# Conditioning vectors of a two-block kernel: second shift and scale as row dot products on VectorE, first gate on TensorE, x loaded feature-major, silu of the conditioning by exp

## The chip, the cores and the metric

One Trainium2 chip; the kernel runs on 1 of its 8 cores. The metric is the device time of one execution in microseconds. The median of three runs of the kernel before is 1270.04 us (1266.39 to 1270.33). The profile is one further execution; its time from the first to the last instruction is called the span.

## The reference

x is 256 tokens by 1024 features, in float32. Only the first block matters here:

```python
cond = silu(c)                                   # c is [1, 1024]
mod = cond @ ada_w + ada_b                       # [1, 6 * 1024]
sh1, sc1, g1, sh2, sc2, g2 = split(mod, 6)
h = rms_norm(x, norm_g[0]) * (1 + sc1) + sh1
x = x + g1 * sb_mixer(h)                         # 16 heads, stick-breaking attention
h = rms_norm(x, norm_g[1]) * (1 + sc2) + sh2
x = x + g2 * hier_moe(h)                         # 32 experts, two for each token
```

The six vectors of the conditioning are products of one row of 1024 with a matrix of 1024 by 6144, 24 MB in all. A second block follows (feed-forward, mixer, feed-forward, last normalization).

## The kernel before

**Tiling.** Activations lie feature-major, as eight tiles of 128 features by 256 tokens. Products that must be exact to float32 are split: a weight w is loaded, ScalarE writes its rounded part wr, VectorE the rest wl = w - wr (split_w), and three matmuls make up for one. Weights come as loads of 1 MB (128 x 2048) into a ring of 15 tiles; the loads are issued by SP's queue in one fixed order, and a load waits until its ring tile is free, with all later loads behind it.

**The first block, in the order of the program.** x is loaded token-major, transposed on TensorE and copied out (L209 to L213); the squares are summed on ScalarE (sq), and the token scales rb spread by two matmuls. cond is a Silu on ScalarE. For each quarter of the features, mod1 forms the first shift and scale (mod_cols: eight matmuls on TensorE with the conditioning as weights, a copy, four transposes, a sum) and then h1; values_quarter makes the values v. Then eight pairs of heads follow, p = 0 to 7: each loads wqk, splits its two halves, makes queries and keys with 48 matmuls (qk), and calls attend for the pair before. attend makes logits z, then takes five passes over 768 columns that alternate: Abs, Exp, Ln on ScalarE, sp on VectorE (L358), the rounded part spr on ScalarE and the rest spl on VectorE (L360), with matmuls of both into z, an Exp, and the product with v; oTr and oTl leave PSUM.

**Conditioning beside the attention.** After the pairs p = 2 to 5, mod_feat(1, p - 2) makes the second shift and scale, and after p = 6 and 7 mod_gate makes the first gate g1, each by mod_cols_ahead: the unit's two loads ada are multiplied by cond, the first on VectorE (four moda passes, L259), the second on GpSimd (L263 to L266: 2048, 1024, 512 and 512 columns), and eight small matmuls add up the partitions.

**After it.** The output product y takes 192 matmuls over the split wo, then come the first residual, the logits of the routing (lt), the routing, and the experts, in eight groups of four. Each group reads 16 loads gu and 8 loads d of 1 MB. The first group's weights are loaded ahead, as far as ring and other tiles have room. The rest of the kernel reads on from the experts' end.

**Order.** Tile's scheduler orders each engine's instructions by its own model of time; engines run their queues in that order and wait for each other by semaphores.

Of the kernel before, what the change touches and what calls it, by code (L numbers as in the profile page):

```python
# [41 lines left out]
def tile_model(ctx: ExitStack, tc: tile.TileContext, a, out, dbg=None):  # L42
# [36 lines left out]
    def hold(name, shape, dt=F32):  # L79
        """A ring tile that takes its place now and not only when its data come."""  # L80
# [33 lines left out]
    zeros = cp.tile([P, 1], F32, name="zeros")  # L114
    V.memset(zeros, 0.0)
# [7 lines left out]
    def rsqrt(v, n, name):  # L123
        """1/sqrt(v) for positive v [128, n]."""
# [63 lines left out]
    def mm_feat(o, wr, wl, hr, hl):  # L188
        """o [128 features, 256] = W^T h, W split [128, 8, 128]."""
# [6 lines left out]
    def mm_tok(o, xr, xl, wr, wl, start, stop):  # L196
        """o [128 tokens, n] += x^T w for one contraction block."""
# [3 lines left out]

    # ---- first normalization
    xT = hold("xT", (P, KT, T))
    for k2 in range(4):
        t = gt(f"xT{k2}", (P, 2, T))
        for tb in range(2):
            for kk in range(2):
# [1094 lines left out]
```

## Time and profile before

| what | value |
|---|---|
| median of three runs | 1270.04 us |
| span of the profiled execution | 1264.9 us |
| PE busy | 1094.0 us (86%) |
| DVE busy | 620.1 us (49%) |
| ACT busy | 450.1 us (36%) |
| POOL busy | 101.4 us (8%) |
| mean granted TensorE clock | 0.938 of full speed |
| HBM traffic | 354.57 MB read |

The page gives no device time of the profiled execution other than its span; the median of the runs is 5.1 us above it. PE is TensorE's matmuls, DVE VectorE, ACT ScalarE, POOL GpSimd, SP the queue that issues the loads. The kernel passes through stretches with different limits: the start and the values to about 51 us, the attention to about 149 us, the output product to about 178 us, routing, the experts from about 191 to 640 us, the second block to the end. Shares of the whole span mix these.

### The profile page before, as it was taken

How to read it: one execution, taken by the hardware profiler on the slowest of the kernel's cores; microseconds unless marked ns; L12 is line 12 of the kernel's file. 1: busy time of each engine (PE TensorE's matmuls, PEld its weight loads, DVE VectorE, ACT ScalarE, POOL GpSimd, SP SyncE). 2: the span in 40 equal slices, each digit the busy share in tenths (PEclk: the TensorE clock that was granted, in tenths of full speed). 3: DMA queues.
4: the chain of work that ended last, by engine and by line, in shares of the span. 5: the costliest groups of instructions: out<-in, count | busy, mean ns of one | idle time of the engine just before them, and what ended most of it. 6: DMA issues, size and time to landing. Idle time of an engine off the chain costs nothing.

```text
span 1264.9 us, 18050 instructions
## 1 busy us (share of the span) xinstructions
PE 1094.0 (86%) x7429; PEld 817.6 (65%) x7429; DVE 620.1 (49%) x1001; ACT 450.1 (36%) x663; POOL 101.4 (8%) x77
## 2 busy tenths in 40 slices
PE   6988988975756776667789999999999999999996
PEld 3787883321312221212179999988988889999995
DVE  4799751210101010101177555577779666755555
ACT  4454641010100000000154444457654555544443
POOL 0277300000000000000020000020000002000001
PEclk9988988989797888978799999999999999999998
DMA  9975688999999999999999440444437656555000
GB/s 382 419 298 219 266 332 357 420 420 420 421 421 418 420 421 421 421 421 422 420 420 370 171 164 1 150 175 159 176 145 296 219 199 250 181 220 182 32 1 34
DMA packets 51354, 356.88 MB, mean 282 GB/s; under 512 B 5824, under 2 KB 6080, under 8 KB 9408
## 3 DMA queue, kind: packets, MB, share of 16 engines
q1 hardware_dynamic: 50400, 353.02, 70.1%
q0 software_dynamic: 576, 2.10, 0.5%
q8 instruction: 61, 1.00, 0.3%
q10 hardware_dynamic: 288, 0.52, 0.1%
q14 instruction: 29, 0.24, 0.1%
HBM read 354.57 MB, written 1.05 MB: 281 GB/s over the span
## 4 chain that ended last, share of the span: by engine, by line
PE 56%; DMA 32%; DVE 7%; issue 2%; ACT 2%; POOL 0%; SPq 0%; ACTq 0%; DVEq 0%
DMA gu<-moe_gu 20%; DMA d<-moe_d 11%; PE fbgu L92 10%; PE fagu L92 9%; PE faacc L92 5%; PE fbacc L92 4%; PE mqk L92 4%; PE mo L92 3%; PE y L92 2%; PE mv L92 2%; PE mz L92 2%; PE mu L92 2%; PE ms L92 2%; PE mg L92 2%; PE gu L92 1%
## 5 line engine op out<-in xcount | busy, mean ns | idle before, releaser
L92 PE MATMUL gu<-gu,xg 128*32 128x512 f32 x1024 | 146.5, 666 | 67.2 <-DMA gu<-moe_gu 67.0
L92 PEld LDWEIGHTS gu<-gu,xg 128*32 128x32 f32 x1024 | 24.8, 113 | 141.0 <-DMA gu<-moe_gu 79.3
L92 PE MATMUL Y<-d,HT 128*32 128x512 f32 (+1 forms) x544 | 83.2, 720 | 26.1 <-DMA d<-moe_d 20.2
L591 DVE TENSOR_SCALAR xg<-xgp,A,mod 128x128 f32<-128x128 f32 x32 | 13.1, 410 | 174.8 <-PE xgp L92 174.8
L656 DVE SCALAR_TENSOR_TENSOR xT<-cmb,g,xT 128x256 f32<-128x256 f32 x60 | 27.8, 484 | 126.4 <-PE cmb L92 126.3
L589 ACT ACTIVATE xg<-xgp,mod,A 128x128 f32<-128x128 f32 x32 | 14.7, 458 | 172.7 <-PE xgp L92 172.7
L92 PEld LDWEIGHTS xgp<-eq,xn 128*128 128x128 f32 x256 | 39.6, 222 | 52.5 <-issue 50.6
L92 PEld LDWEIGHTS Y<-d,HT 128*32 128x32 f32 x544 | 15.5, 126 | 78.7 <-DMA d<-moe_d 50.4
L92 PE MATMUL xgp<-eq,xn 128*128 128x128 f32 x256 | 49.3, 329 | 8.0 <-DVE eq L579 7.1
L650 ACT ACTIVATE Ys<-Y 128x512 f32<-128x512 f32 x15 | 9.0, 597 | 120.0 <-PE Y L92 120.0
L92 PE MATMUL cmb<-CT,Ys 128*128 128x256 f32 x128 | 41.1, 452 | 11.3 <-ACT Ys L650 10.3
L92 PEld LDWEIGHTS cmb<-CT,Ys 128*128 128x128 f32 x128 | 24.9, 217 | 36.7 <-ACT Ys L650 25.3
L849 POOL TENSOR_TENSOR faq<-faq,faq 128x256 f32<-128x256 f32 x10 | 9.3, 951 | 460.6 <-ACT faq L845 460.4
L612 DVE TENSOR_TENSOR H<-H,gu 128x512 f32<-128x512 f32 x8 | 5.5, 688 | 66.7 <-ACT H L611 66.7
L263 POOL TENSOR_TENSOR ada<-ada,cond 128x2048 f32<-128x2048 f32 x6 | 24.5, 4079 | 33.9 <-DMA ada<-ada 33.9
L611 ACT ACTIVATE H<-gu 128x512 f32<-128x512 f32 x8 | 4.8, 597 | 60.2 <-PE gu L92 60.2
L970 DVE SCALAR_TENSOR_TENSOR cv<-cs,pk,cv 128x255 f32<-128x255 f32 (+2 forms) x48 | 22.3, 477 | 0.4
L615 PEld LDWEIGHTS HTp<-kc,H 128*128 128x128 f32 x32 | 4.8, 188 | 25.3 <-DVE H L612 25.3
L782 DVE TENSOR_TENSOR fbsc<-fbgu,rb 128x512 f32<-128x512 f32 x22 | 15.0, 691 | 10.9 <-PE fbgu L92 10.8
L782 DVE TENSOR_TENSOR fasc<-fagu,rb 128x512 f32<-128x512 f32 x22 | 15.0, 690 | 10.5 <-PE fagu L92 10.5
L1204 POOL TENSOR_TENSOR fin<-x,final_norm_g 128x512 f32<-128x512 f32 x4 | 5.1, 1281 | 180.2 <-issue 177.2
L264 POOL TENSOR_TENSOR ada<-ada 128x1024 f32<-128x1024 f32 x6 | 19.1, 3184 | 0.2
(2266 smaller groups left out, 3608.2 us busy)
## 6 DMA issues: line engine op xcount, KB each, us to landing
gu<-moe_gu SPq DMA_DIRECT2D x127, 1024.0 KB, 19.8
d<-moe_d SPq DMA_DIRECT2D x60, 1024.0 KB, 19.8
ada<-ada SPq DMA_DIRECT2D x24, 1024.0 KB, 10.6
fawi<-f1i SPq DMA_DIRECT2D x21, 1024.0 KB, 17.4
fbwi<-f2i SPq DMA_DIRECT2D x21, 1024.0 KB, 4.8
fawo<-f1o SPq DMA_DIRECT2D x11, 1024.0 KB, 14.2
fbwo<-f2o SPq DMA_DIRECT2D x11, 1024.0 KB, 4.8
wqk<-sbqk SPq DMA_DIRECT2D x8, 1024.0 KB, 16.4
```

The source lines that it names most:

```text
L92: return PE.matmul(o, l, r, start=start, stop=stop, **kw)
L263: G.tensor_tensor(w4, w4, cond[:, 4:8, None].to_broadcast([P, 4, 512]), ALU.mult)
L264: G.tensor_tensor(w[:, 0:1024], w[:, 0:1024], w[:, 1024:2048], ALU.add)
L589: S.activation(xg[:, k, :], t, AF.Identity, scale=A2[:, k:k + 1], bias=sh2[:, k:k + 1])
L591: V.tensor_scalar(xg[:, k, :], t, A2[:, k:k + 1], sh2[:, k:k + 1], ALU.mult, ALU.add)
L612: V.tensor_tensor(H, H, gu[:, 1, :], ALU.mult)
L650: S.activation(Ys, Y, AF.Copy)
L656: V.scalar_tensor_tensor(xT[:, kt, :], c[:, kk, :], g2[:, kt:kt + 1], xT[:, kt, :], ALU.mult, ALU.add)
L782: V.tensor_tensor(gu, ps, rb[:, None, :].to_broadcast([P, 2, T]), ALU.mult)
L849: (V if i and kt > 3 else G).tensor_tensor(sums[i], sums[i], s_, ALU.add)
L970: V.scalar_tensor_tensor(cv[:, d:T], ts[:, 0:T - d], pk[:, cw + 3 - d:cw + 4 - d], cv[:, d:T], ALU.mult, ALU.add)
L1204: G.tensor_tensor(z[:, half(hf)], xs, fn[:, half(hf)], ALU.mult)
```

## The change

Five edits, all ahead of the experts.

1. **Second shift and scale.** The matrix is loaded transposed (adar, eight loads of 1 MB, one for each 128 output features, with the 1024 inputs along the columns). A new tile crow holds c, broadcast to all 128 partitions by one DMA of 512 KB, and its silu. Each of the sixteen outputs of 128 features is one VectorE pass over 1024 columns that multiplies and sums (mod_row, accum_out). One adar load and two such passes follow each pair of heads p = 0 to 7. mod_rows_end adds the bias and forms A2 for all features at once.
2. **First gate.** mod_gate(0, h) goes through mod_cols on TensorE, after p = 3 and p = 5. mod_cols_ahead is gone, and with it all its work on GpSimd and VectorE.
3. **x** is loaded feature-major straight into xT; the transposes are gone. The sums of squares come from two ScalarE passes over 1024 columns, one VectorE sum and four matmuls with ones, and lie on all partitions at once, so that rsqrt runs on 128 x 256 in place of 128 x 2.
4. **silu** is c / (1 + exp(-c)), for cond (128 x 8) and crow (128 x 1024): an Exp on ScalarE, an addition, a reciprocal and a product on VectorE. The table for Exp and Ln is loaded first; the Silu table and the second load of it at the start are gone.
5. The first loads are pk, xT, kc in place of kc, x, pk.

```diff
+    set_exp = S.preload_act_table_set("natural_log_exp_and_others")
+    def silu_of(dst, src, e):
+        with tc.issue_after(set_exp.ins):
+            S.activation(e, src, AF.Exp, scale=-1.0)
+        V.tensor_scalar(e, e, 1.0, None, ALU.add)
+        V.reciprocal(e, e)
+        V.tensor_tensor(dst, src, e, ALU.mult)
...
-    def mod_cols_ahead(u, name):
-        acc = acp.tile([P, 512], F32, tag="acc", name=f"moda{name}")
-        ws = [load(a["ada"][u, r], f"ada{u}{r}") for r in range(2)]
-        for j in range(4):
-            V.scalar_tensor_tensor(acc, ws[0][:, 512 * j:512 * j + 512], cond[:, j:j + 1],
-                                   acc if j else zeros.to_broadcast([P, 512]), ALU.mult, ALU.add)
-        w = ws[1]
-        w4 = w.rearrange("p (j n) -> p j n", j=4)
-        G.tensor_tensor(w4, w4, cond[:, 4:8, None].to_broadcast([P, 4, 512]), ALU.mult)
-        G.tensor_tensor(w[:, 0:1024], w[:, 0:1024], w[:, 1024:2048], ALU.add)
-        G.tensor_tensor(w[:, 0:512], w[:, 0:512], w[:, 512:1024], ALU.add)
-        G.tensor_tensor(acc, acc, w[:, 0:512], ALU.add)
...
+    def mod_row(kt):
+        if not crow:
+            c = w8("crow", (P, 2, D))
+            nc.sync.dma_start(c[:, 0], bass.AP(tensor=a["c"].tensor, offset=a["c"].offset, ap=[[0, P], [1, D]]))
+            silu_of(c[:, 0], c[:, 0], c[:, 1])
+            crow.append(c)
+        c = crow[0]
+        w = load(a["adar"][kt], f"adar{kt}")
+        for j in range(2):
+            V.scalar_tensor_tensor(c[:, 1], w[:, D * j:D * j + D], 1.0, c[:, 0], ALU.mult, ALU.mult,
+                                   accum_out=mod[:, 1, j, kt:kt + 1])
...
-        if 1 < p < 6:
-            mod_feat(1, p - 2)
-        elif p > 5:
-            mod_gate(0, p - 6, mod_cols_ahead)
+        mod_row(p)
+        if p in (3, 5):
+            mod_gate(0, p // 2 - 1)
     attend(*pend)
+    mod_rows_end()
```

On VectorE, in the middle of the attention, the kernel before has this order (z_611 and z_720 are the logits of the first two pairs of heads, sp and spl the passes of attend, wqk40l the rest of a split weight):

```order
L386 SCALAR_TENSOR_TENSOR qkl_717<-qk_691,qkr_716 128x256
L168 TENSOR_TENSOR wqk40l<-wqk_910,wqk40r 128x1024
L277 TENSOR_TENSOR mod<-modt_774,pk 128x2x2
L259 SCALAR_TENSOR_TENSOR moda_890<-ada_891,cond,zeros 128x512
L279 SCALAR_TENSOR_TENSOR A_174<-mod,pk 128x2
L259 SCALAR_TENSOR_TENSOR moda_890<-ada_891,cond,moda_890 128x512 x2
L358 SCALAR_TENSOR_TENSOR sp_721<-z_720,sp_721 128x768
L259 SCALAR_TENSOR_TENSOR moda_890<-ada_891,cond,moda_890 128x512
L168 TENSOR_TENSOR wqk41l<-wqk_910,wqk41r 128x1024
L386 SCALAR_TENSOR_TENSOR qkl_813<-qk_787,qkr_812 128x256
L360 TENSOR_TENSOR spl_723<-sp_721,spr_722 128x768
```

In the changed kernel the same place on VectorE reads (z_704 is the second pair's z, crow,mod<-adar a row product):

```order
L278 SCALAR_TENSOR_TENSOR crow,mod<-adar_745,crow 128x1024
L363 SCALAR_TENSOR_TENSOR sp_705<-z_704,sp_705 128x768
L278 SCALAR_TENSOR_TENSOR crow,mod<-adar_858,crow 128x1024
L391 SCALAR_TENSOR_TENSOR qkl_781<-qk_755,qkr_780 128x256
L169 TENSOR_TENSOR wqk40l<-wqk_885,wqk40r 128x1024
L278 SCALAR_TENSOR_TENSOR crow,mod<-adar_858,crow 128x1024
L169 TENSOR_TENSOR wqk41l<-wqk_885,wqk41r 128x1024
L365 TENSOR_TENSOR spl_707<-sp_705,spr_706 128x768
L391 SCALAR_TENSOR_TENSOR qkl_814<-qk_788,qkr_813 128x256
L278 SCALAR_TENSOR_TENSOR crow,mod<-adar_994,crow 128x1024
```

The passes of 512 columns that fed GpSimd's sum have given way to row products of 1024 columns, which stand ahead of sp, spl and the splits.

On TensorE, where the fourth pair's queries begin, the kernel before has (z_720 is the second pair's, z_611 the first pair's logits, qk_787 the fourth pair's queries):

```order
L92 MATMUL z_720<-qkl_575,qkr_607 128x256 x2
L92 MATMUL z_720<-qkl_575,qkr_607 128x128 x2
L92 MATMUL z_720<-qkr_574,qkl_608 128x256 x2
L92 MATMUL z_611<-spr_613,ntri 128x384
L92 MATMUL z_611<-spr_613,nones 128x128
...
L92 MATMUL z_720<-qkr_574,qkl_608 128x128 x2
L92 MATMUL modt_774<-ones,moda_761 128x1 x4
L92 MATMUL qk_787<-h1r,wqk30r 128x256
```

In the changed kernel TensorE has, behind the fourth pair's keys qk_788 and ahead of the fifth pair's queries qk_891 (mod_psg is the first gate):

```order
L94 MATMUL qk_788<-h1r,wqk31l 128x256
L94 MATMUL mod_psg_862<-ada_863,cond_104 32x512 x4
L94 MATMUL mod_psg_862<-ada_869,cond_104 32x512 x4
L94 MATMUL z_704<-spr_706,ntri 128x384
...
L94 MATMUL z_591<-sp_592,v 64x256 x2
L94 MATMUL z_591<-sp_592,v 64x128 x2
L94 MATMUL z_704<-spl_707,ntri 128x384
...
L94 MATMUL z_817<-spr_819,ntri 128x384
...
L94 MATMUL z_817<-spl_820,ntri 128x384
...
L94 MATMUL qk_891<-h1r,wqk40r 128x256
```

Before, each attend is spread among the queries and keys of the next pair; now the scheduler puts the attends of the pairs 2 and 3, and of 4 and 5, one behind the other, with no queries and keys between them. From the output product on, the order on every engine is that of before, but for a few neighbours that change places.

## Rows read from the trace of the kernel before

**Rows 1.** The page's chain that ended last, by line.
```profile
DMA gu<-moe_gu 20%; DMA d<-moe_d 11%; PE fbgu L92 10%; PE fagu L92 9%; PE faacc L92 5%; PE fbacc L92 4%; PE mqk L92 4%; PE mo L92 3%; PE y L92 2%; PE mv L92 2%; PE mz L92 2%; PE mu L92 2%; PE ms L92 2%; PE mg L92 2%; PE gu L92 1%
```
**Rows 2.** Windows: stretch, length, busy of PE, PEld, DVE, ACT, POOL; PEclk, DMA, GB/s.
```profile
80.00:90.00 10.00, 7.08 (x54) 6.22 (x54) 9.96 (x11) 3.94 (x7) 6.18 (x3) 0.98 0.24 80
90.00:100.00 10.00, 10.00 (x65) 8.80 (x65) 9.22 (x9) 4.14 (x6) 7.66 (x3) 0.66 0.62 243
190.00:200.00 10.00, 10.00 (x73) 3.90 (x75) 1.56 (x6) 1.37 (x3) 0.00 (x0) 0.84 0.58 224
260.00:640.00 380.00, 261.74 (x1589) 88.17 (x1589) 46.34 (x101) 34.49 (x69) 1.42 (x2) 0.85 1.01 421
```
**Rows 3.** The chain that ended last, in order of time: start, length, what.
```profile
20.41 1.90 PE mod_ps L92 x16
...
102.77 2.04 DVE spl L360
...
146.10 1.22 PE z L92 x16
147.31 1.01 PE cb L92 x8
148.33 0.80 PE z L92 x8
...
165.25 0.52 PE z L92 x4
...
170.40 7.85 PE y L92 x65
...
241.59 14.94 DMA gu<-moe_gu
```
**Rows 4.** Groups by form, 0 to 240 us: busy us, mean ns, idle before.
```profile
L263 POOL TENSOR_TENSOR ada<-ada,cond 128x2048 f32<-128x2048 f32 x6 | 24.5, 4079 | 33.9 <-DMA ada<-ada 33.9
...
L259 DVE SCALAR_TENSOR_TENSOR moda<-ada,cond,zeros 128x512 f32<-128x512 f32 x4 | 11.2, 2810 | 0.0
...
L259 DVE SCALAR_TENSOR_TENSOR moda<-ada,cond,moda 128x512 f32<-128x512 f32 x12 | 9.0, 748 | 0.1
...
L168 DVE TENSOR_TENSOR wqk01l<-wqk,wqk01r 128x1024 fp32r<-128x1024 f32 x1 | 4.1, 4124 | 1.5 <-ACT wqk01r L166 1.5
...
L168 DVE TENSOR_TENSOR wv0l<-wv,wv0r 128x1024 fp32r<-128x1024 f32 x1 | 1.2, 1226 | 0.0
```
**Rows 5.** Single lines of VectorE: duration in ns, least, median and most.
```profile
L360 DVE TENSOR_TENSOR spl<-sp,spr x8: 950/1692/2794, 74.5 to 161.3; 128x768 fp32r<-128x768 f32 x8
...
L279 DVE SCALAR_TENSOR_TENSOR A<-mod,pk x8: 147/160/3554, 23.3 to 124.3; 128x2 f32<-128x2 f32 x8
...
L1051 DVE RECIPROCAL dn<-dn x8: 152/160/165, 899.7 to 959.6; 128x1 f32<-128x1 f32 x8
...
L550 DVE RECIPROCAL gden<-gden x1: 167/167/167, 189.7 to 189.7; 128x2 f32<-128x2 f32 x1
```
**Rows 6.** Groups by form, 0 to 240 us: further passes of the attention.
```profile
L358 DVE SCALAR_TENSOR_TENSOR sp<-z,sp 128x768 f32<-128x768 f32 x8 | 7.6, 952 | 2.8 <-ACT sp L357 2.8
L356 ACT ACTIVATE sp<-sp 128x768 f32<-128x768 f32 x8 | 6.7, 844 | 0.2
...
L386 DVE SCALAR_TENSOR_TENSOR qkl<-qk,qkr 128x256 fp32r<-128x256 f32 x16 | 6.6, 413 | 0.0
```
**Rows 7.** Instructions in order of time: start, length, engine and line.
```profile
5.95 0.19 ACT L144 ACTIVATION_READ_ACCUMULATOR rms_j<-x 128x1 f32 x1
...
19.59 1.06 ACT L166 ACTIVATE wv0r<-wv 128x1024 fp32r<-128x1024 f32 x1 [5.14 <-DMA wv<-sbv]
...
23.53 0.60 ACT L295 ACTIVATE h1r<-xs,mod,A 128x256 fp32r<-128x256 f32 x1 [1.93 <-DVE A L279]
...
49.42 1.23 DVE L168 TENSOR_TENSOR wqk00l<-wqk,wqk00r 128x1024 fp32r<-128x1024 f32 x1 [0.55 <-ACT wqk00r L166]
```
**Rows 8.** DMA from 78 to 200 us.
```profile
DMA packets 5022, 31.34 MB, mean 257 GB/s; under 512 B 562, under 2 KB 562, under 8 KB 1842
```

More of the change, by code (lines that the diff above doesn't have):

```diff
@@ L123, in rsqrt @@
     def rsqrt(v, n, name):
+        sm = t1 if n == T else small
         i = sm(name + "_i", (P, n), I32)
@@ L200, in mm_tok @@
         return mm(o, xl, wr, False, stop)
[L203 to L207, printed above, removed]
-                k = 2 * k2 + kk
-                PE.transpose(t[:, kk, tb * P:(tb + 1) * P], x[:, tb, k * P:(k + 1) * P], ident)
-        if k2 % 2:
-            S.activation(xT[:, 2 * k2:2 * k2 + 2, :], t, AF.Copy)
-        else:
-            V.tensor_copy(xT[:, 2 * k2:2 * k2 + 2, :], t)
-    ss = sm("ss1", (P, 2, 2))
-    for tb in range(2):
-        for hf in range(2):
-            sq(x[:, tb, half(hf)], ss[:, tb, hf:hf + 1], f"rms1{tb}{hf}")
-    r1 = rms_finish(ss, "rms1")
-    rb = cp.tile([P, T], F32, name="rb")
-    spread(r1, "r1")
-    ins = S.activation(cond, pk[:, PK_C:PK_C + KT], AF.Silu)
-    with tc.issue_after(ins.ins):
-        set_exp = S.preload_act_table_set("natural_log_exp_and_others")
-    V.tensor_copy(cond32, cond[:, :, None].to_broadcast([P, KT, 32]))
+    set_exp = S.preload_act_table_set("natural_log_exp_and_others")
[5 more added lines that the diff above has]
+        V.tensor_tensor(dst, src, e, ALU.mult)
+    cpk = pk[:, PK_C:PK_C + KT]
+    silu_of(cond, cpk, sm("ce", (P, KT)))
+    V.tensor_copy(cond32, cond[:, :, None].to_broadcast([P, KT, 32]))
+    sqx = [t4(f"sqx{i}") for i in range(2)]
+    for i in range(2):
+        with tc.issue_after(set_exp.ins):
+            S.activation(sqx[i], xT[:, 4 * i:4 * i + 4, :].rearrange("p k t -> p (k t)"), AF.Square, scale=1.0 / 32)
+    V.tensor_tensor(sqx[0], sqx[0], sqx[1], ALU.add)
+    t = gt("ss1", (P, T))
+    for k in range(4):
+        mm(t, ones, sqx[0][:, T * k:T * k + T], k == 0, k == 3)
+    v1 = t1("ss1v")
+    V.tensor_scalar(v1, t, RMS_EPS, None, ALU.add)
+    rb = cp.tile([P, T], F32, name="rb")
+    V.tensor_copy(rb, rsqrt(v1, T, "rms1"))
     mod = cp.tile([P, 2, 2, KT], F32, name="mod")
@@ new lines, in tile_model @@
+    crow = []
+    def mod_row(kt):
[9 more added lines that the diff above has]
+                                   accum_out=mod[:, 1, j, kt:kt + 1])
@@ L281, in tile_model, with mod_rows_end, mod_gate @@
+    def mod_rows_end():
+        b = pk[:, PK_AB + 16:PK_AB + 32].rearrange("p (j c) -> p j c", j=2)
+        V.tensor_tensor(mod[:, 1], mod[:, 1], b, ALU.add)
+        V.scalar_tensor_tensor(A2, mod[:, 1, 1], 1.0, pk[:, PK_G2:PK_G2 + KT], ALU.add, ALU.mult)
     g1 = cp.tile([P, KT], F32, name="g1")
     g2 = cp.tile([P, KT], F32, name="g2")
-    def mod_gate(i, h, cols):
-        m4 = cols(8 + 2 * i + h, f"g{i}{h}")
+    def mod_gate(i, h):
+        m4 = mod_cols(4 + 2 * i + h, f"g{i}{h}")
         ks, c = slice(4 * h, 4 * h + 4), PK_AG + 8 * i + 4 * h
@@ L1256, in layouts @@
     aw = f("ada_w")[0].reshape(2, 4, P, 6, D)
-    un = [aw[:, :, :, i:i + 2, 256 * h:256 * h + 256] for i in (0, 3) for h in range(4)]
+    un = [aw[:, :, :, 0:2, 256 * h:256 * h + 256] for h in range(4)]
     un += [aw[:, :, :, i:i + 1, 512 * h:512 * h + 512] for i in (2, 5) for h in range(2)]
     A["ada"] = np.stack([m.transpose(0, 2, 1, 3, 4).reshape(2, P, 2048) for m in un])
+    A["adar"] = f("ada_w")[0].T.reshape(6, KT, P, D)[3:5].transpose(1, 2, 0, 3).reshape(KT, P, 2048)
     w = f("sb_w_in")[0]
```

36 lines of the change are left out of this document (16 added, 20 removed).

## The prediction

> **What bounds the kernel now.** I began with the page's chain by line: a third of it is the experts' transfers, gu 20% and d 11%, and the rest is mostly TensorE [rows 1]. The chain in time says where these stand: from 241.59 us on it is transfers [rows 3], and from 260 to 640 us the DMA moves 421 GB/s at a busy share of 1.01 while TensorE works 262 of 380 us [rows 2]. There a cheaper vector on VectorE saves nothing, and the second block keeps its order. All five edits lie before 180 us, so they count only as far as the experts' transfers end earlier. Do they? From 78 to 200 us the DMA moved 31.34 MB [rows 8]; at the 421 GB/s of the full stretch that takes 74.4 us, so it stood 47.6 us idle, and in the last 10 us of that it was at 0.58 [rows 2]. The loads ahead wait for tiles that the attention and the output product free, not for bandwidth. Hence the end of the output product (the last y begins at 170.40 and takes 7.85, so 178.25 [rows 3]) carries the experts' stream with it, 1:1, as long as the gain stays far under 47 us.
>
> So the question is what sets 178.25. The windows say VectorE: from 80 to 90 us it is busy 9.96 of 10 us and TensorE 7.08 [rows 2], and the chain passes through spl in this stretch (102.77, 2.04 us) [rows 3]. The groups by form show why. The split pass wv0l takes 1.226 us, the same pass on wqk01l 4.124; a pass of moda takes 0.748, its first pass, reading zeros, 2.810 [rows 4]. spl takes 0.950 to 2.794, A of two columns 0.147 to 3.554 [rows 5]. The long ones have all their operands in SBUF and lie where GpSimd multiplies ada (4.079 us for one pass [rows 4]); passes with an operand in PSUM, as qkl (0.413) and sp (0.952), keep one duration [rows 6]. My reading: a pass of VectorE and one of GpSimd hold each other up there. And TensorE pays twice: after the stretch where it had gaps its granted clock is 0.66 from 90 to 100 us, so partly at 1.2 in place of 2.4 GHz [rows 2], 3.4 us of 10.
>
> **The change part by part.** *Start (x feature-major, silu by Exp).* Transposes and table loads go, but the values need wv too: its first split begins when the load lands, 19.59, and takes 1.06; two of these must pass before h1 is at 21.7 at the earliest, where h1r stands at 23.53 after 1.93 us of waiting on A [rows 7]. The gain is 0 to 1.9; I take 1.5, since mod_cols (20.41, 1.90 [rows 3]) still stands before A. The new rsqrt on 256 columns lies in the wait for wv. So VectorE comes to the first queries' split at 49.42 − 1.5 = 47.9 [rows 7].
>
> *GpSimd's work away.* Splits, spl and A fall back to the undisturbed 1.226, 0.950 and 0.15 us. Sums of squares, A2 and the bias stay small and lie in idle time.
>
> *Row products in place of moda.* Sixteen passes of 1024 columns, on VectorE, ahead of sp and spl in its queue: what stands behind them are the splits for TensorE's next queries and the spl that attend waits for. None is in this trace. From below: the split of 1024 columns with two SBUF operands, 1.226. From above as the usual case: 0.06 more for the form (0.748 against half of 1.226 at 512 columns is 0.135 a pass, but part of it is the start) and 0.19 for handing out the sum, as ScalarE's accumulator takes [rows 4, 7]: 1.48. I take 1.4. Two passes over the columns would be 2.6; that is a rival. Their loads (adar, 8 MB) replace the 8 MB of ada for the second shift and scale; crow adds 512 KB, 1.2 us in 47 idle ones, and one ring tile until about 115 us.
>
> *silu of crow.* An Exp of 1024 columns on ScalarE ahead of wqk01r: 1.06 as the pass of that size [rows 7]; VectorE then waits 1.5 for wqk01r as it did [rows 4] and 1.06 more. Then an addition, a reciprocal and a product of 1024 columns. Addition and product 1.226 each. The trace has reciprocals of one column (0.152 to 0.165) and of two (0.167) [rows 5], so a column costs between nothing visible and 15 ns, 15.4 us for 1024. Since two columns cost what A of two columns costs (0.160), I take 1.226; the middle is a rival.
>
> *First gate on TensorE.* Twice 1.90 for the products and 0.52 for four transposes (as z x4), where the old way had twenty-four small matmuls for six units: about even; counted below.
>
> *The sum* goes by the order of the changed kernel. VectorE from 47.9 to the end of the third pair's spl: waits 2.6; eleven splits at 1.226, 13.5; silu of crow 3.7; ten passes of PSUM at 0.413, 4.1; three sp at 0.952, 2.9; three spl at 0.950, 2.9; twelve row products at 1.4, 16.8. That is 46.4, and spl ends at 94.3 (before, the spl at 102.77 ended at 104.8 [rows 3], but TensorE was one pair of heads further by then, so the difference isn't the gain). From there VectorE has less per pair than TensorE, which has left: 192 matmuls of queries and keys at 7.85/65 = 0.121, 23.2; as many of y, 23.2; for the third pair 0.52 and 0.80, for the fourth 0.52, 0.52, 0.80; four whole attends of 1.22, 0.52, 0.52, 0.80, together 12.2; the first gate's transposes 0.52 and the second's 1.90 and 0.52; the routing's cb twice 1.01 [rows 3]. Sum 66.7, so 161.0. Two things come on top. The scheduler puts the attends of pairs 4 and 5 one behind the other, with 3.1 us for TensorE (gate 1.90, z 1.22) beside a chain of four ScalarE passes at 0.844, sp 0.952 and spl 0.950 [rows 3, 5, 6], 5.3: about 2 us. And gaps stay before 94, so once more the 3.4 us of the low clock. The output product ends at 166.4, 11.9 us earlier. Span 1264.9 − 11.9 = 1253.0. The profiled execution's span is 5.1 under the median of the runs; with the same 5.1 the forecast is **1258 us**. A run can tell 0.3%, 3.8 us, from no change, so faster means under 1266.2 and slower over 1273.9.
>
> **The rivals.** *The reciprocal is slow.* At half of 15 ns per column, 1024 columns take 7.7 and add 6.5 us to VectorE before spl, with wqk01l and all later splits queued behind it: gain 5.4, **1264.6**. For it: nothing in rows but the 15 ns between the fastest of one column and that of two; against it: the medians differ by 7. The Trainium skill, *VectorE: DVE Perf Modes*, First, the fixed hardware budget, says that the reciprocal is an iterative division with a repeat count of 8; at eight times the time of a column in the split pass that would be, as an estimate from that page, up to 9.8 us, and by it the gain would be about 3 us. No row here shows it.
>
> *The row products take two passes: slower.* A product of 1024 columns then costs twice 1.226 and 0.19, 2.6: 1.2 more each, 14.4 over the twelve before the third spl. TensorE meanwhile has more gaps and loses another 3.4 us to the lower clock: 14.4 + 3.4 − 11.9 = 5.9 later, **1276**. It decides from 2.4 us per product (1.4 + 11.9/12), where the gain is gone. For it: they stand on the one engine that is full here. Against it: moda's pass also reads two SBUF tiles and takes 0.748 for 512 columns, not 1.2 [rows 4], though it hands out no sum. The Trainium skill, *Vector Engine (DVE) Microarchitecture Reference*, Points that are easy to get wrong, speaks for it: this form with two SBUF sources that aren't bf16 halves its rate, as no port is left to read an accumulator back. The trace shows no halving without the sum; with it no row tells.
>
> *The gain doesn't arrive.* Loads leave SP's queue in one order, and if wo or the experts' first weights wait for something else than tiles freed by the attention, the DMA's end stays: about **1270**. Against it speaks the idle share of 0.58 just when the experts begin [rows 2].
>
> *Better.* If the gaps before 94 us close (VectorE's rows shorter, the attends in pairs free of cost), TensorE alone sets the end: without the 3.4 and the 2, and with the row products at 1.226 (another 2.1), the gain is 19.4: **1250.6**.
>
> **How the numbers follow.** Forecast 0.52; slow reciprocal 0.20; two passes 0.12; no arrival 0.08; better 0.08. The forecast's own spread is about 6 us, from the start (0 to 1.9), the row products (1.226 to 1.48: 3 us over twelve) and the clock (0 to twice 3.4): 1252 to 1264. The range takes in the better case's middle and the slow reciprocal to its far side, and leaves out most of the two passes: 1249 to 1270. Faster: nearly all of the forecast (0.51), the better case (0.08), and three quarters of the slow reciprocal (0.15), 0.74. Slower: the two passes, and a little for a reciprocal at its upper end, 0.13. The same: 0.13.
>
> **What the changed kernel's profile would show.** GpSimd near idle from 50 to 145 us, and every split at about 1.23 and spl at 0.95: if they still spread, the reading of GpSimd falls. The row products' mean, against 1.4 and 2.44; the reciprocal's one row, against 1.2 and 7.7; the third spl's end at 94; y's end at 166; the experts' first products at 179, and the last transfers of the experts 12 us earlier with stages of the same length behind. The forecast is wrong if TensorE's gaps between 60 and 95 us last longer than the sum allows, if its granted clock stays at the low level beyond 10 us, or if the experts' stream does not move with y.

## The result

The changed kernel takes **1252.48 us** (median of four runs, 1250.84 to 1253.52) beside 1270.18 (1266.39 to 1271.38) of the kernel before: a ratio of 0.987, with a 95% interval of 0.9851 to 0.9889. It is faster by 17.7 us by the medians and by 16.5 by the ratio, more than the 12 that were forecast, and inside the range. Its profiled execution has a span of 1251.7 us, where the sum of the prediction came to 1253.0.

The page's chain by line, of the changed kernel. The transfers gu and d are still its largest single item with TensorE behind; the share of gu is smaller than in [rows 1] because the chain is followed back only to 399.6 us here:

```profile
DMA gu<-moe_gu 11%; PE fbgu L94 10%; PE fagu L94 9%; DMA d<-moe_d 6%; PE faacc L94 5%; PE fbacc L94 4%; PE mqk L94 4%; PE mo L94 3%; PE mv L94 2%; PE mz L94 2%; PE mu L94 2%; PE ms L94 2%; PE mg L94 2%; PE sc L94 0%; PE nu L94 0%
```

Windows of the changed kernel, with the columns of [rows 2]: stretch, length, busy of PE, PEld, DVE, ACT, POOL; granted clock, DMA share, GB/s.

```profile
80.00:90.00 10.00, 8.83 (x79) 5.97 (x79) 9.40 (x14) 5.79 (x10) 0.00 (x0) 1.00 0.85 332
90.00:100.00 10.00, 7.07 (x41) 6.92 (x42) 7.50 (x12) 6.57 (x8) 0.00 (x0) 0.66 0.96 401
...
170.00:180.00 10.00, 7.11 (x43) 6.73 (x42) 7.00 (x41) 2.91 (x7) 0.88 (x2) 0.56 0.74 297
...
240.00:620.00 380.00, 266.59 (x1607) 88.92 (x1595) 43.19 (x95) 31.08 (x61) 0.00 (x0) 0.84 1.01 423
```

GpSimd is gone from the attention. TensorE still has a gap, which now lies mostly from 90 to 100 us (busy 7.07 of 10) and not from 80 to 90, and the mean clock of 90 to 100 us is again 0.66. From 110 to 120 us TensorE idles 1.7 us, where in the kernel before it idled 5.0. And the transfers of the experts run at 423 GB/s, where [rows 2] has 421.

Single lines of VectorE in the changed kernel: duration in ns, least, median and most, and when:

```profile
L278 DVE SCALAR_TENSOR_TENSOR crow<-adar,crow x16: 1215/1218/1226, 63.8 to 107.4; 128x1024 f32<-128x1024 f32 x16
...
L365 DVE TENSOR_TENSOR spl<-sp,spr x8: 948/958/960, 75.2 to 147.1; 128x768 fp32r<-128x768 f32 x8
...
L210 DVE RECIPROCAL crow<-crow x1: 6553/6553/6553, 51.1 to 51.1; 128x1024 f32<-128x1024 f32 x1
...
L169 DVE TENSOR_TENSOR wqk01l<-wqk,wqk01r x1: 1160/1160/1160, 57.6 to 57.6; 128x1024 fp32r<-128x1024 f32 x1
```

spl, which spread from 0.95 to 2.79 us [rows 5], has one duration; wqk01l takes 1.16 in place of 4.12 [rows 4]. A row product takes 1.218. The reciprocal of 1024 columns takes 6.55, so the size that a rival gave it (7.7) was nearer than the forecast's 1.2.

Three points show where the 13.2 us between the two spans were won: the last matmul of the output product, the experts' first product (gu) and their last one (Y). Start, length and instruction, in the kernel before, then in the changed one:

```profile
177.97 0.28 PE L92 MATMUL y<-oTr,wo7l 128*128 128x256 f32 x1
...
190.86 3.01 PE L92 MATMUL gu<-gu,xg 128*32 128x512 f32 x16
...
637.42 1.07 PE L92 MATMUL Y<-d,HT 128*32 128x256 f32 x16 [1.30 <-DMA d<-moe_d]
```
```profile
168.16 0.28 PE L94 MATMUL y<-oTr,wo7l 128*128 128x256 f32 x1
...
182.02 3.30 PE L94 MATMUL gu<-gu,xg 128*32 128x512 f32 x16
...
626.07 1.07 PE L94 MATMUL Y<-d,HT 128*32 128x256 f32 x16 [1.21 <-DMA d<-moe_d]
```

The output product ends 9.8 us earlier; the routing gives 1 us back, under a granted clock of 0.56 from 170 to 180 us; the experts end 11.3 us earlier, so 2.5 us come in their own stretch; and the second block is 1.9 us shorter.

### The profile page after: what moved, and what is told of

Its sections match the earlier page's. It is cut to its first block, busy times and chain, and to the rows that moved or that the text cites. A ratio compares the mean times of both kernels' runs of the same rounds, so it can differ in the third digit from the quotient of the medians.

```text
span 1251.7 us, 17974 instructions
## 1 busy us (share of the span) xinstructions
PE 1091.1 (87%) x7409; PEld 811.9 (65%) x7409; DVE 596.9 (48%) x1009; ACT 448.1 (36%) x654; POOL 35.0 (3%) x52
## 4 chain that ended last, share of the span: by engine, by line
PE 47%; DMA 17%; DVE 2%; ACT 1%; issue 0%; POOL 0%; SPq 0%; DVEq 0%; ACTq 0%
DMA gu<-moe_gu 11%; PE fbgu L94 10%; PE fagu L94 9%; DMA d<-moe_d 6%; PE faacc L94 5%; PE fbacc L94 4%; PE mqk L94 4%; PE mo L94 3%; PE mv L94 2%; PE mz L94 2%; PE mu L94 2%; PE ms L94 2%; PE mg L94 2%; PE sc L94 0%; PE nu L94 0%
## 5 line engine op out<-in xcount | busy, mean ns | idle before, releaser
L94 PE MATMUL cmb<-CT,Ys 128*128 128x256 f32 x128 | 41.0, 451 | 11.3 <-ACT Ys L655 10.3
L278 DVE SCALAR_TENSOR_TENSOR crow<-adar,crow 128x1024 f32<-128x1024 f32 x16 | 19.5, 1218 | 0.1
L620 PE MATMUL HTp<-kc,H 128*128 128x128 f32 x32 | 7.7, 386 | 13.1 <-DVE H L617 13.1
L614 ACT ACTIVATE CT<-ctp 128x256 f32<-128x256 f32 x8 | 3.1, 385 | 31.6 <-PE ctp L612 31.6
```

Of the source, the lines that this page charges most:

```text
L94: return PE.matmul(o, l, r, start=start, stop=stop, **kw)
L278: V.scalar_tensor_tensor(c[:, 1], w[:, D * j:D * j + D], 1.0, c[:, 0], ALU.mult, ALU.mult, accum_out=mod[:, 1, j, kt:kt + 1])
L620: PE.transpose(ht[:, f, :], H[:, f * P:(f + 1) * P], ident)
```

## The experiments

Each ran beside the kernel before on the same chip. The column "first gu" is the start of the experts' first product in the profile, the first point behind everything that the change touches.

| kernel | median us | ratio to before, interval | first gu | span |
|---|---|---|---|---|
| before (profile of [rows 1 to 8]) | 1270.18 | 1 | 190.86 | 1264.9 |
| changed | 1252.48 | 0.987, 0.9851 to 0.9889 | 182.02 | 1251.7 |
| before_again | 1268.77 | 0.9999, 0.9985 to 1.0013 | 192.31 | 1266.7 |
| after_again | 1251.42 | 0.9862, 0.9843 to 0.9881 | 181.32 | 1251.3 |
| gpsimd_back | 1274.54 | 1.0044, 1.0028 to 1.0061 | 204.25 | 1273.8 |
| all_vector | 1258.76 | 0.9918, 0.9898 to 0.9937 | 184.63 | 1257.8 |
| all_tensor | 1264.2 | 0.9961, 0.9946 to 0.9976 | 187.86 | 1266.3 |
| start_old | 1254.27 | 0.9889, 0.9873 to 0.9906 | 181.02 | 1252.3 |
| rows_twice | 1252.84 | 0.9882, 0.9862 to 0.9902 | 180.19 | 1250.5 |
| no_reciprocal | 1251.2 | 0.9863, 0.9846 to 0.9879 | 179.24 | 1248.7 |
| gates_early | 1250.96 | 0.9864, 0.9847 to 0.988 | 176.76 | 1248.9 |
| gate_rows | 1241.6 | 0.9786, 0.977 to 0.9802 | 170.33 | 1240.3 |
| before_c | 1268.05 | 0.9991, 0.9977 to 1.0005 | 190.92 | 1263.6 |

**The two kernels again.** before_again and after_again are the kernels as they stand.

> The kernel before once more, beside itself: a ratio of 1.000 with an interval of some 0.2% to each side, which says what a difference the later runs can tell. Its profile shows whether an execution near the median (1270) differs from the profiled one (span 1264.9, where the time beside the span can't be 5.1 us if the changed kernel's is 1.8): if so, the 4 to 5 us lie in one stretch or in one rate. I expect them in the experts' stretch, as a lower rate of the transfers (419 in place of 421 GB/s is 2.2 us over 400 us), and not ahead of 180 us.

> The changed kernel once more, beside the runs of this batch: 1252.5, ratio 0.987. It says what a difference of the two kernels below to it is worth; I expect 1.5 us of scatter of one execution. Its time beside the span is 1.8 us, as in every run that has both.

The ratios repeat. The profiled execution of before_again took 1268.54 us with a span of 1266.7, that of the changed kernel 1253.52 with 1251.7: 1.8 us lie around the span in both. With 1.8 us the profile of [rows 1 to 8] would belong to an execution of 1266.7, near the lowest of its runs. And what parts it from before_again's, whose span is 1.8 us longer, is not the transfers (421 GB/s in both) but 1.5 us that are there by the first gu: in before_again TensorE is busy 5.70 us from 80 to 90 and gets a clock of 0.51 behind it, in place of 7.08 and 0.66 [rows 2]. The expectation had the place wrong.

**GpSimd put back.** The changed kernel, its instructions in the same order on TensorE, VectorE, ScalarE and SP's queue, with passes of GpSimd beside them that write a tile nobody reads:

```diff
             V.scalar_tensor_tensor(c[:, 1], w[:, D * j:D * j + D], 1.0, c[:, 0], ALU.mult, ALU.mult,
                                    accum_out=mod[:, 1, j, kt:kt + 1])
+        if kt > 1:
+            s = acp.tile([P, 512], F32, tag="acc", name=f"gs{kt}")
+            for j in range(8):
+                G.tensor_tensor(s, w[:, 512 * (j % 4):512 * (j % 4) + 512], w[:, 0:512], ALU.mult)
```

> The changed kernel with passes on GpSimd added beside six of the row products' loads: each multiplies 512 columns of the adar tile into a scratch tile that nothing reads, eight passes for each of p = 2 to 7. No other instruction is added or moved on any engine. If GpSimd's work and VectorE's passes on SBUF hold each other up, splits and row products beside it go from 1.22 to up to 4 us again, spl from 0.95 to a median near 1.7, sp and qkl stay at 0.95 and 0.42, and the kernel falls back by most of what it gained: 12 to 20 us, about 1265 to 1272. If the stretching of before came from elsewhere (transfers into SBUF, the form of moda), the passes keep their times and the kernel stays within 2 us of 1252.

Measured 1274.54: all of the gain is gone and 5 us more. The windows from 50 to 140 us of before, of the changed kernel and of gpsimd_back (columns as above) show that GpSimd is busier here than it was before, 81.8 us against 65.3, and that TensorE has the fewest matmuls (the count behind its busy time) in gpsimd_back, though it has the changed kernel's order:

```profile
50.00:140.00 90.00, 79.24 (x594) 72.64 (x592) 87.14 (x78) 46.21 (x64) 65.27 (x23) 0.91 0.69 276
```
```profile
50.00:140.00 90.00, 83.23 (x672) 74.38 (x672) 69.57 (x97) 53.34 (x76) 0.00 (x0) 0.94 0.82 320
```
```profile
50.00:140.00 90.00, 67.62 (x500) 58.53 (x498) 87.79 (x81) 39.80 (x56) 81.81 (x43) 0.87 0.65 255
```

Groups by form of this kernel, 40 to 180 us (busy us, mean ns, idle before):

```profile
L283 POOL TENSOR_TENSOR gs<-adar 128x512 f32<-128x512 f32 x48 | 88.8, 1849 | 43.7 <-DMA adar<-adar 40.0
...
L278 DVE SCALAR_TENSOR_TENSOR crow<-adar,crow 128x1024 f32<-128x1024 f32 x16 | 32.4, 2027 | 0.1
...
L369 DVE TENSOR_TENSOR spl<-sp,spr 128x768 fp32r<-128x768 f32 x8 | 10.7, 1338 | 4.0 <-ACT spr L368 4.0
...
L367 DVE SCALAR_TENSOR_TENSOR sp<-z,sp 128x768 f32<-128x768 f32 x8 | 7.6, 950 | 3.2 <-ACT sp L366 1.8 <-PE y L94 1.5
...
L210 DVE RECIPROCAL crow<-crow 128x1024 f32<-128x1024 f32 x1 | 6.6, 6553 | 0.0
...
L395 DVE SCALAR_TENSOR_TENSOR qkl<-qk,qkr 128x256 fp32r<-128x256 f32 x16 | 6.5, 412 | 0.0
```

Passes with two operands in SBUF stretch (row product 1.22 to 2.03, spl 0.96 to 1.34), those with one operand in PSUM (sp, qkl) or one operand in all (the reciprocal) don't. This is the pattern of [rows 4 to 6], made on purpose. The other reading, that GpSimd's reads keep the adar tiles longer and so hold up the loads behind them, does not fit: in this kernel no wait of SP's queue from 40 to 200 us ends with GpSimd, and the longest waits of TensorE from 45 to 180 us are for VectorE's and ScalarE's passes, none for a load. The longest of them, with us in total, times and the longest single one:

```profile
PE z L94 <- DVE spl L369: 8.1, 2, 6.5
```

The long passes also show how the two engines hold each other up. In the kernel before, A of two columns begins inside a GpSimd pass and ends where that pass ends, at 113.3 us (start, length):

```profile
109.26 4.05 POOL L263 TENSOR_TENSOR ada<-ada,cond 128x2048 f32<-128x2048 f32 x1
...
109.77 3.55 DVE L279 SCALAR_TENSOR_TENSOR A<-mod,pk 128x2 f32<-128x2 f32 x1
```

All the long ones do this: from 45 to 170 us the 23 stretched passes of before and the 36 of gpsimd_back end within 0.2 us of the end of a GpSimd pass plus their own undisturbed time. So such a pass waits until GpSimd's pass has ended; it does not run slower beside it. The Trainium skill, *SBUF — State Buffer*, SBUF: two separate sides, describes it as an exclusive lock on a port pair that VectorE's passes with two SBUF inputs and GpSimd's passes share, held for a whole instruction. The trace agrees, with A's 3.55 us beside the pass of 4.05.

**Without GpSimd, by two other ways.** Both start from the kernel before. In all_vector the half that GpSimd made becomes four more moda passes:

```diff
-        w4 = w.rearrange("p (j n) -> p j n", j=4)
-        G.tensor_tensor(w4, w4, cond[:, 4:8, None].to_broadcast([P, 4, 512]), ALU.mult)
...
-        G.tensor_tensor(acc, acc, w[:, 0:512], ALU.add)
+        for j in range(4):
+            V.scalar_tensor_tensor(acc, w[:, 512 * j:512 * j + 512], cond[:, 4 + j:5 + j], acc, ALU.mult, ALU.add)
```

> The kernel before with one edit: the second half of each ada product, GpSimd's, becomes four more moda passes of 512 columns on VectorE. If GpSimd's presence is the cost, VectorE loses the 38 us by which its passes were stretched and gets 24 x 0.75 = 18 us: 20 us less on the engine that sets 51 to 140 us, splits at 1.22, and a time near 1258 to 1262 although VectorE has more to do. If the gain of the change came from the row products or the start, this is no faster than before, or slower by up to 18 us.

Measured 1258.76, 10 us under before, although VectorE has 24 passes more. The first pass, on zeros, falls from 2.81 [rows 4] to 0.745, spl to 0.951:

```profile
L357 DVE TENSOR_TENSOR spl<-sp,spr 128x768 fp32r<-128x768 f32 x8 | 7.6, 951 | 0.5 <-ACT spr L356 0.5
...
L259 DVE SCALAR_TENSOR_TENSOR moda<-ada,cond,zeros 128x512 f32<-128x512 f32 x4 | 3.0, 745 | 0.0
```

In all_tensor all six units go through mod_cols:

```diff
-        m4 = (mod_cols, mod_cols_ahead)[i](4 * i + qt, f"{i}{qt}")
+        m4 = mod_cols(4 * i + qt, f"{i}{qt}")
...
-            mod_gate(0, p - 6, mod_cols_ahead)
+            mod_gate(0, p - 6, mod_cols)
```

> The kernel before with mod_cols on TensorE for all six units that were made ahead: no GpSimd, no moda on VectorE, no row products. VectorE loses the stretching and all 18 us of moda; TensorE gets 6 x 2.4 us and loses 48 small matmuls. If it is only GpSimd's presence that cost, and TensorE has gaps to take the products, the time is near the changed kernel's, 1253 to 1258. If the row products on VectorE are what pays, it stays nearer to all_vector's 1259 or above, with TensorE full and a later output product.

Measured 1264.2, over all_vector: here TensorE is the full engine, and what goes to it is paid. (The profile is of its slowest execution, 1268.06.) Two windows of all_tensor, TensorE at 10 of 10 us and VectorE at 6.5 and 4.8:

```profile
110.00:120.00 10.00, 10.00 (x86) 8.22 (x86) 6.46 (x11) 6.23 (x10) 0.00 (x0) 1.00 0.70 271
...
130.00:140.00 10.00, 10.00 (x86) 7.72 (x79) 4.81 (x9) 5.66 (x8) 0.00 (x0) 1.00 0.75 279
```

So of the 17 us some 10 come from taking GpSimd's passes away with the work left on VectorE (5 with the work on TensorE). What is left between all_vector and the changed kernel is 6.1 us of span, in these two profiles: 2.6 at the first gu, where the row products, the gate on TensorE and the new order weren't taken apart; 2.6 in the experts' stretch, where all_vector's transfers run at 421 GB/s; and 0.9 in the second block.

**The start put back.**

```diff
-    set_exp = S.preload_act_table_set("natural_log_exp_and_others")
...
-    silu_of(cond, cpk, sm("ce", (P, KT)))
+    xT = hold("xT", (P, KT, T))
...
+                PE.transpose(t[:, kk, tb * P:(tb + 1) * P], x[:, tb, k * P:(k + 1) * P], ident)
...
+    ins = S.activation(cond, pk[:, PK_C:PK_C + KT], AF.Silu)
```

> The changed kernel with the start of before put back: x token-major with the transposes, the Silu and its table load for cond, the old order of the first loads; the silu of crow, the row products and the first gate stay. In the changed kernel VectorE comes to the first queries' split at 49.24, in the kernel before at 49.42, and the transfers are at 413 to 427 GB/s from 10 to 50 us in both. If the transfers set the start, this kernel is within 1 us of the changed one (1252 to 1253). My sum gave the start 1.5 us; if that is right, it shows 1.5 us and a split that begins at 50.7.

Measured 1254.27, which is 1.8 and 2.9 us over the two medians of the changed kernel. But the profile does not put this at the start: the first gu comes at 181.02, 0.3 and 1 us earlier than in the changed kernel's two profiles, the first queries' split begins at 48.54, not at 50.7, and the experts end at 625.55, as in after_again (625.60). The 1.0 us by which its span is longer than after_again's lies behind the last matmul of the kernel (11.1 us from there to the end against 10.0); the rest of the difference is not in the profiled executions. So no gain of the start was found where it was forecast, and why this kernel is slower stays open. A window of the changed kernel, and two of start_old, show transfers at their full rate in both.

```profile
40.00:50.00 10.00, 9.37 (x46) 6.70 (x39) 8.43 (x15) 4.99 (x6) 0.00 (x0) 1.00 1.02 423
```
```profile
10.00:20.00 10.00, 5.81 (x33) 2.04 (x35) 4.28 (x17) 4.53 (x7) 0.20 (x2) 1.00 1.01 424
...
40.00:50.00 10.00, 9.37 (x45) 7.28 (x42) 9.07 (x16) 5.78 (x7) 0.00 (x0) 1.00 1.02 427
```

**VectorE's load doubled and cut.** rows_twice makes each row product a second time; no_reciprocal makes the silu of crow on ScalarE:

```diff
+            V.scalar_tensor_tensor(c[:, 1], w[:, D * j:D * j + D], 1.0, c[:, 0], ALU.mult, ALU.mult,
+                                   accum_out=sm("again", (P, 1)))
```
```diff
-            silu_of(c[:, 0], c[:, 0], c[:, 1])
+            with tc.issue_after(set_exp.ins):
+                S.activation(c[:, 1], c[:, 0], AF.Exp, scale=-1.0)
+            S.activation(c[:, 1], c[:, 1], AF.Ln, bias=1.0)
+            S.activation(c[:, 1], c[:, 1], AF.Exp, scale=-1.0)
+            V.tensor_tensor(c[:, 0], c[:, 0], c[:, 1], ALU.mult)
```

> The changed kernel with each row product made twice, the second time with its sum into a scratch column: 16 more passes of 1.22, 12 of them ahead of the third spl, at a pitch of 1.14 us some 13.7 us there. This is the price that the slower rival would have had (about 2.4 us a product). If VectorE's rows set the end, as my sum has it, the kernel is 9 to 14 us slower, 1262 to 1266, and the third spl ends near 106. If VectorE has slack in the changed kernel, because TensorE and the attend's own chain of passes set the end, it is under 4 us slower.

> The changed kernel, where the silu of crow comes from three passes of ScalarE (Exp, Ln of one more, Exp of the negative) and one product on VectorE: the addition (0.69) and the reciprocal (6.55) on VectorE go, two passes of about 1.06 are added on ScalarE. If VectorE's rows up to the third spl still set the end, as my sum has it, the third spl ends 5 to 7 us earlier and the kernel is 4 to 6 us faster, about 1247. If TensorE and the attend's own chain of passes set it by now (TensorE waits 0.9 us for wqk01l in the changed kernel and 2.9 for spr at 93.7), the gain is under 2 us.

Neither moved the time by what my sum had said: 1252.84 and 1251.2, beside 1251.42 and 1252.48 of the changed kernel. In no_reciprocal VectorE has 7.2 us less to do, and the third spl starts at 92.15 in place of 93.71. In rows_twice it starts at 94.48, but here the scheduler moved passes back: 14 and not 24 stand ahead of that spl, the last at 132 us (in the changed kernel 12, the last at 107). So rows_twice shows that VectorE has room for 16 passes more by 132 us, at no price in the time; what twelve slow ones would cost in the old places it doesn't show. Windows of rows_twice, then of no_reciprocal:

```profile
90.00:100.00 10.00, 5.80 (x36) 5.50 (x32) 9.93 (x18) 5.94 (x8) 0.00 (x0) 0.66 0.65 271
100.00:110.00 10.00, 10.00 (x84) 9.15 (x83) 9.97 (x18) 5.24 (x9) 0.00 (x0) 1.00 0.68 232
110.00:120.00 10.00, 8.47 (x75) 6.28 (x75) 9.98 (x17) 6.78 (x10) 0.00 (x0) 0.91 0.89 348
```
```profile
80.00:90.00 10.00, 7.71 (x70) 4.37 (x62) 7.33 (x12) 5.19 (x9) 0.00 (x0) 1.00 1.00 411
90.00:100.00 10.00, 7.97 (x45) 7.42 (x46) 5.93 (x12) 5.38 (x8) 0.00 (x0) 0.66 0.60 229
```

With VectorE at 9.9 or at 6 to 7 of 10 us, TensorE has a gap of 4 to 5 us from 80 to 100 us and the same low clock behind it. From the first queries' split to the end of the third spl VectorE idles 1.8 us in the changed kernel and 7.6 in no_reciprocal. The gap isn't VectorE's load. The changed kernel's timeline (start, length, engine and line, and in brackets the idle time and what ended it) names its chain:

```profile
89.15 0.81 ACT L360 ACTIVATE sp<-z 128x768 f32<-128x768 f32 x1 [0.32 <-PE z L94]
90.00 0.85 ACT L361 ACTIVATE sp<-sp 128x768 f32<-128x768 f32 x1
90.87 0.84 ACT L362 ACTIVATE sp<-sp 128x768 f32<-128x768 f32 x1
...
92.83 0.84 ACT L364 ACTIVATE spr<-sp 128x768 fp32r<-128x768 f32 x1 [1.12 <-DVE sp L363]
...
93.71 0.96 DVE L365 TENSOR_TENSOR spl<-sp,spr 128x768 fp32r<-128x768 f32 x1 [0.91 <-ACT spr L364]
...
93.73 0.69 PE L94 MATMUL z<-spr,ntri 128*128 128x384 f32 x1 [2.93 <-ACT spr L364]
```

Abs, Exp, Ln, sp, spr and spl follow each other, VectorE itself waits 0.91 us for spr, and TensorE waits 2.93. The likely reason is that the scheduler has put two attends one behind the other there, with no queries and keys between them; the next two kernels bear on it.

**The order, and TensorE's work.** Both kernels start from no_reciprocal. In gates_early the gate's units follow p = 1 and 2, and the later attends lie among queries and keys again. gate_rows makes the first gate, too, by row products (its matrix comes transposed, in four loads adag), so that mod_cols leaves the attention altogether:

```diff
-        if p in (3, 5):
-            mod_gate(0, p // 2 - 1)
+        if p in (1, 2):
+            mod_gate(0, (1, 2).index(p))
```
```diff
+    def gate_row(i):
+        c = crow[0]
+        w = load(a["adag"][i], f"adag{i}")
+        for j in range(2):
+            V.scalar_tensor_tensor(c[:, 1], w[:, D * j:D * j + D], 1.0, c[:, 0], ALU.mult, ALU.mult,
+                                   accum_out=g1[:, 2 * i + j:2 * i + j + 1])
...
-        if p in (3, 5):
-            mod_gate(0, p // 2 - 1)
+        if p in (4, 5, 6, 7):
+            gate_row((4, 5, 6, 7).index(p))
```

> no_reciprocal with the first gate's two units after p = 1 and p = 2 in place of p = 3 and p = 5. The scheduler then spreads the attends of the later pairs among queries and keys of the next pairs, where no_reciprocal (and the changed kernel) has two attends one behind the other twice, with gaps of TensorE from 80 to 100 us (4.3 us) and from 110 to 120 (1.7), each followed by a low granted clock (0.66 from 90 to 100). If these pairs of attends are what TensorE waits for now, the gaps and the low clock after them go, and the time is 3 to 7 us under no_reciprocal's, 1244 to 1248. If the loads of the gate, 4 MB earlier in SP's queue, come ahead of wqk and delay it, TensorE waits for splits of wqk instead and the time is 1251 or more.

> no_reciprocal with the first gate, too, as row products on VectorE (eight more passes of 1.22, one load for two of them after each of p = 4 to 7, the bias at the end): TensorE loses the gate's 2 x 1.90 us of products and 2 x 0.52 us of transposes. Since twice the row products cost nothing, VectorE has room for eight more, and if TensorE's own work sets the end of the output product, that end comes 4 to 5 us earlier than in no_reciprocal (lt at 162 in place of 166.7) and the time is 1246 to 1248. If the gain is eaten on the way (the routing at a low granted clock, the experts' stream that waits for tiles, as gates_early's 4.1 us at lt became nothing at the end), the time is 1250 or more.

gates_early: the gaps of 80 to 100 us go, but now the logits of the first two attends stand one behind the other at 64 to 68 us, with only the gate's first unit between them, and the gap comes behind them. TensorE waits 5.3 us for spr, whose sp stands on VectorE behind two splits and a row product; the mean clock of 70 to 80 us is 0.66. Windows from 60 to 100 us:

```profile
60.00:70.00 10.00, 8.12 (x79) 6.33 (x77) 4.08 (x7) 5.05 (x7) 0.00 (x0) 1.00 1.01 424
70.00:80.00 10.00, 6.55 (x40) 6.02 (x40) 8.64 (x14) 5.84 (x7) 0.00 (x0) 0.66 1.01 424
80.00:90.00 10.00, 10.00 (x89) 7.79 (x88) 8.98 (x16) 5.18 (x9) 0.00 (x0) 1.00 0.85 344
90.00:100.00 10.00, 10.00 (x85) 10.00 (x84) 8.91 (x16) 6.07 (x9) 0.00 (x0) 1.00 1.02 428
```

So the gap is where two attends follow each other, in the changed kernel and here. The output product ends 4.1 us earlier than in no_reciprocal (its last matmul at 162.44 against 166.54), the experts begin 2.5 us earlier and end 1.8 us earlier, and the time doesn't follow at all (1250.96 against 1251.2; expected 1244 to 1248). The last part of the loss can be seen: behind the experts' end its clock is low where no_reciprocal's isn't, at a mean of 0.83 for 20 us. First gates_early, then no_reciprocal:

```profile
621.00:641.00 20.00, 17.97 (x131) 16.67 (x132) 13.18 (x19) 12.83 (x22) 8.69 (x8) 0.83 1.02 423
```
```profile
623.00:643.00 20.00, 17.84 (x148) 16.51 (x149) 14.81 (x28) 12.71 (x22) 8.70 (x8) 1.00 1.01 425
```

gate_rows: **1241.6 us**, 10 us under the changed kernel, the best of all, and more than the expected 1246 to 1248. The gap from 80 to 100 us and the low clock are gone, two gaps of 0.9 and 0.8 us at 110 to 120 stay, and VectorE carries eight passes more:

```profile
80.00:90.00 10.00, 10.00 (x90) 9.32 (x88) 9.26 (x15) 6.06 (x10) 0.00 (x0) 1.00 0.96 383
90.00:100.00 10.00, 10.00 (x87) 9.06 (x87) 10.00 (x18) 6.39 (x10) 0.00 (x0) 1.00 0.91 329
100.00:110.00 10.00, 10.00 (x84) 9.55 (x84) 9.13 (x13) 6.58 (x9) 0.00 (x0) 1.00 0.85 306
110.00:120.00 10.00, 8.29 (x76) 7.46 (x74) 9.64 (x20) 5.62 (x10) 0.00 (x0) 1.00 0.99 381
```

The gate's own work is 4.8 us of TensorE, by the rows of before; the other half of the gain likely comes from the order that comes about without it. These two weren't taken apart.

**The place of the inputs.**

```diff
+    A["c"] = f("c")[0]
...
+    nc.sync.dma_start(cdum, bass.AP(tensor=a["c"].tensor, offset=a["c"].offset, ap=[[0, 1], [1, 8]]))
```

> The kernel before with one more input of 4 KB (c, of which 32 bytes are loaded at the start and not used), so that the inputs behind it may lie elsewhere in memory, as in the changed kernel; no instruction of an engine is moved. In all kernels that have the changed kernel's inputs (six so far) the experts' transfers ran at 423 GB/s, in the four with those of before at 421. If the place of the inputs sets this, the rate is 423 here and the time 2 to 3 us under that of before, 1266 to 1267; otherwise 421 and 1269.

The rate rose to 423 GB/s, with the order on TensorE, VectorE and ScalarE that of before but for one memset at the start. The transfers from 260 to 600 us, of before_again, then of before_c:

```profile
DMA packets 19621, 143.01 MB, mean 421 GB/s; under 512 B 2179, under 2 KB 2179, under 8 KB 2179
```
```profile
DMA packets 19739, 143.88 MB, mean 423 GB/s; under 512 B 2190, under 2 KB 2190, under 8 KB 2190
```

Its first gu comes at 190.92, as before, and its last d product at 634.65 in place of 637.42: 2.8 us in the experts' stretch, of which the second block gives 1.5 back (628.9 us from there to the end against 627.4). In the median the difference is under 1 us and not resolved. That it is the place of the inputs in memory is a guess: the extra input also brings a load of 32 bytes and a small tile in SBUF, and the three weren't taken apart.

## Why the prediction held, and where it did not

**What bounds the kernel: right.** VectorE stretched by GpSimd set 51 to 140 us. gpsimd_back and all_vector show it from both sides, and the changed kernel's splits at 1.22 and spl at 0.96 are what the text said they would be.

**The start: 1.5 us forecast, nothing found.** The first queries' split moved from 49.42 [rows 7] to 49.24. The step that failed looked at the waits around h1 and not at the windows of 10 to 50 us of the kernel before, in which the transfers run at 413 to 427 GB/s: it seems that whatever is ready earlier waits for the next weights. The longer time of start_old is not explained by this.

**Row products and reciprocal: both mis-sized, in opposite directions.** A product took 1.218, its read of the sum 0.083, and the next pass starts before either has ended, so that one costs 1.14 in the queue in most places and not 1.4. The reciprocal took 6.55 and not 1.23, 6.4 ns a column. The rows had this: the medians of one column and of two differ by 7 ns [rows 5], which makes 7.2 us for 1024. The step that failed set this aside, counted the 7 ns as evidence against a slow reciprocal, and followed the likeness with A, whose two columns take as long as the reciprocal's. The Trainium skill's rule on the reciprocal (*VectorE: DVE Perf Modes*, First, the fixed hardware budget) had the direction right: 6.55 is 5.3 times a split pass, under the estimate of eight times. The Trainium skill's rule on products with a sum (*Vector Engine (DVE) Microarchitecture Reference*, Points that are easy to get wrong) does not show here: 1.218 us for 1024 columns with two float32 sources in SBUF and a sum is the time of a plain split pass.

**The sum of VectorE's queue: right number by luck, wrong reason.** The third spl ended at 94.67, forecast 94.3. The errors cancelled: 1.3 us at the start and 5.3 of the reciprocal too little, 3.1 of twelve row products too much, and the rest because waits were shorter and passes of VectorE overlap a little at their ends. And the sum held that VectorE's rows set this point, and no_reciprocal shows that they don't: 7.2 us less gave 1.6 there, of which 0.8 were won ahead of the first queries' split. With GpSimd gone, TensorE, its order of the attends and the passes of one attend set the end; VectorE is close behind them, since in gpsimd_back, where all its passes grow in the old order, the third spl slips to 113.0. The rival of the slow reciprocal (1264.6) was priced by the same step and falls with it: the reciprocal did turn out slow, and taking its 6.6 us away changed the median by 0.2 to 1.3 us. The rival of two passes over the columns did not come about; its price stays untested.

**TensorE from there on.** Forecast 72.1 us (66.7, 2 for the paired attends, 3.4 of clock) from the third spl to the end of y; measured 73.6. The gap before 94 us and the low clock behind it came as the sum had them, 2.93 us of waiting for spr and a mean clock of 0.66 from 90 to 100; the pair of attends at 110 to 120 us cost TensorE 1.7, where the sum had 2.

**One to one to the end.** Roughly, for this change: 9.8 us at y, 8.8 at the first gu, 11.3 at the experts' end, 13.2 at the end. As a rule it does not hold: of the 4.1 us that gates_early won at y nothing was left at the end. Two things were not in the sum. The transfers run 0.5% faster, 2.5 us, which before_c shows with the extra input alone and none of the edits; and the second block is 1.9 us shorter, which I can't derive from the edits: 0.9 us of it come in the first 30 us behind the experts, where the order of a few neighbours differs, and 0.6 behind the last matmul. Both helped a forecast whose y was 2 us too early, so the total is nearer than the steps.

**From span to time.** I added 5.1 us, the distance of the span to the median of before. The time around a span is 1.8 us; the other 3.3 were the distance of one quick execution to the median. With 1.8 the forecast would have been 1254.8. That is more than half of its miss.

## What to carry to other kernels

Two engines that work on SBUF side by side may be slower than one alone: look for passes of one form with two durations, and for what runs beside the long ones. When that is taken away, ask anew which engine is full: here it was TensorE, so the work that is best moved next is TensorE's onto the engine that has just got room (gate_rows, another 10 us), not the longest pass on that engine. And before a sum of one engine's rows is trusted as a bound, name the wait that ends at its last row.

## What the runs showed of the hardware that was not expected

- A reciprocal of 128 x 1024 float32 took 6.55 us on VectorE, of 128 x 8 0.20, of 128 x 1 0.16 [rows 5]: the small sizes hide the cost of a column.
- A product of two float32 tiles in SBUF with a sum over 1024 columns took 1.218 us, no more than the product alone.
- With one more input of 4 KB and a 32-byte load of it the experts' transfers ran at 423 GB/s and not at 421, with the engines' instructions those of before but for one memset that changed its place. The reason stays open.
- A VectorE pass with two operands in SBUF waited for the end of a GpSimd pass: 59 such passes in two kernels end within 0.2 us of that end plus their own time.
- The clock that TensorE was granted was 0.66 in the mean of 90 to 100 us in the changed kernel, no_reciprocal and rows_twice, where TensorE had idled 2 to 4.2 us of that window. In the changed kernel it is 0.50, the level of 1.2 GHz, from 93 to 99 us, behind the wait of 2.93 us and while TensorE is busy all the time from 94 on, and 1.00 again from 100. In gate_rows, with gaps of 0.9 and 0.8 us at 110 to 120, it stayed at 1.00, 2.4 GHz, from 40 to 160 us.
